# Moving a 128-byte filling tile in a Trainium2 decoder trunk: the weight pool against the pools of the moving operands

## The chip, the cores and the metric

The kernel runs on one core of one Trainium2 chip. The metric is the device time of one execution in microseconds; of several executions the median is taken. Lower is better.

## The reference

One decoder layer over a sequence of 1024 tokens and a width of 1024, all in float32:

```python
hn = rms_norm(h, norm_mix_g)
proj = hn @ w_in                      # width 10256, split into za, zb, zc, xbc, dt_raw, g_raw
ya = gmlp_mixer(za, ...)              # gated MLP over positions, in chunks of 128
yb = rg_lru_mixer(zb, ...)            # convolution, gates, linear recurrence
yc = ssd_mixer(zc, xbc, dt_raw, ...)  # Mamba-2 style chunked scan
gates = sigmoid(g_raw + b_gate)       # three gates of width 1024
merged = gates[0]*(ya @ w_branch_a) + gates[1]*(yb @ w_branch_b) + gates[2]*(yc @ w_branch_c)
h = h + merged @ w_out
hn = rms_norm(h, norm_mlp_g)
h = h + (relu(hn @ w_mlp_up)**2) @ w_mlp_down     # hidden width 4096
return rms_norm(h, final_norm_g)
```

## The kernel before

**How a product is made.** Each float32 operand is cut into a high part and a rest (`split`, lines 132 and 133: ScalarE copies the source into an fp32r tile, VectorE subtracts that from the source). A product of two operands is three fp32r matmuls on TensorE: high by high, high by rest, rest by high. Each matmul has a stationary operand of 128 by 128, brought in by a weight load of its own (the PEld rows of the profile), and a moving operand of mostly 128 by 512, streamed from SBUF. The sum is collected in PSUM. In the profile's names, `out<-moving,stationary`.

**The stages in order of time.** (1) The rows of x are normed and transposed into the `xn` pool, and the second half of za is projected with x as the stationary operand (`v_matmuls`, line 257). (2) 34 projections with a 128-column weight tile each (`wtile`, `product`, line 564): the weight's two parts come from the pool `w`, the moving operand from `xn`; the three mixers run beside them. (3) The other input projections in pairs of weight tiles by a seven-product scheme (`Pair`, `seventh`, line 487). (4) The three branch products and the gated merge (`merge_product`, line 487). (5) The output projection (`out_products`, line 1387). (6) The MLP's first product (`Super`, line 487, and `plain`, line 1647). (7) Its second product (`dn_product`, line 487), then the last norm and the stores.

```python
 46    base = ctx.enter_context(tc.tile_pool(name="base", bufs=1))
 47    wp = ctx.enter_context(tc.tile_pool(name="w", bufs=6))
 48    rawp = ctx.enter_context(tc.tile_pool(name="raw", bufs=2))
 49    small = ctx.enter_context(tc.tile_pool(name="small", bufs=1))
...
 58    xp = normed.enter_context(tc.tile_pool(name="xn", bufs=16, side="right"))
 60    pools = [acts.enter_context(tc.tile_pool(name="act", bufs=15))]
 62    halfp = mixers.enter_context(tc.tile_pool(name="half", bufs=16))
...
 84    sm(SPACER, "spacer")
...
487                mm(ps, lhs[l][kk], rhs[r][kk], start=(new and n == 0), stop=(n == 11), skip_group_check=not new)
...
564                    mm(ps[:, hsl(h)], w[wi][:, k, :], a.rhs(ai, k, h), start=(n == 0), stop=(n == 3 * KD - 1))
...
1387                mm(ps, M.tok(a, k, c), wo[nb][k][w], start=(k == 0 and a + w == 0), stop=(k == KD - 1 and a == 1))
```

**What lies where in SBUF.** The pools are stacked in the order of the code, from the left; `xn`, and `act3` in its place later, are stacked from the right end. `base` holds the identity, the ones and some columns. `w` has six tiles and `raw` two, of 4096 bytes in each partition: `w` holds weights that are already split (names `wh`, `wl`, `wt`, `wb`), `raw` holds weights as they are loaded (`raw`, `rt`). `small` holds columns of a few bytes; its first tile is `spacer`, 32 float32 values (128 bytes in each partition) that no instruction reads or writes. Behind `small` come `act`, `half`, `lruw` and `const`; later `act1`, `act2` and `actx` take the places of some of these. With the sizes in the code the pools start at these bytes of a partition:

| pool | tile names | start | start modulo 256 | modulo 512 |
|---|---|---|---|---|
| `base` | `ident`, `ones`, ... | 16512 | 128 | 128 |
| `w` | `wh`, `wl`, `wt`, `wb` | 18656 | 224 | 224 |
| `raw` | `raw`, `rt` | 43232 | 224 | 224 |
| `small`, without the spacer | ... | 51552 | 96 | 352 |
| `act`, `act2` | `a` | 52704 | 224 | 480 |
| `half`, `act1` | `h`, `c` | 114144 | 224 | 480 |
| `lruw`, `actx` | `lw`, `x` | 146912 | 224 | 480 |
| `xn`, `act3` | `xn`, `b` | 163808 | 224 | 480 |

The tiles of the large pools are 2048 or 4096 bytes long (`lruw`: 1024), and a 128-column operand within them starts at a multiple of 512 bytes.

**What sets the order.** Large parts of the program are written out in order by hand (`manual_schedule`), the rest is ordered by the framework from the data that each instruction needs. No address enters into that order.

Of the kernel before, what the change touches and what calls it, by code (L numbers as in the profile page):

```python
# [8 lines left out]
F32 = mybir.dt.float32  # L9
# [7 lines left out]
P = 128  # L17
# [13 lines left out]
SPACER = 32  # L31
# [5 lines left out]
def trunk_kernel(ctx: ExitStack, tc: tile.TileContext, x, norm_mix_g, w_in, b_gate, gmlp_ln_g, gmlp_ln_b,  # L37
# [6 lines left out]
    w_out, w_up, w_dn = w_out[0], w_mlp_up[0], w_mlp_down[0]  # L44

    base = ctx.enter_context(tc.tile_pool(name="base", bufs=1))
    wp = ctx.enter_context(tc.tile_pool(name="w", bufs=6))
    rawp = ctx.enter_context(tc.tile_pool(name="raw", bufs=2))
    small = ctx.enter_context(tc.tile_pool(name="small", bufs=1))
# [18 lines left out]
    def nm(s):  # L68
        uid[0] += 1
        return f"{s}_{uid[0]}"  # L70
# [10 lines left out]
    def sm(n, tag, dt=F32, bufs=None):  # L81
        return small.tile([P, n], dt, tag=tag, name=nm(tag), bufs=bufs)

    sm(SPACER, "spacer")

    tt = nc.vector.tensor_tensor
    stt = nc.vector.scalar_tensor_tensor
# [197 lines left out]
    with tc.manual_schedule():  # L285
# [16 lines left out]
        for c in range(2, NCH):  # L302
# [8 lines left out]
                                base=0, channel_multiplier=-1)  # L311
# [78 lines left out]
        for c in range(1, NCH):  # L390
# [23 lines left out]
            if c == 4:  # L414
                nc.gpsimd.affine_select(out=wT, in_=wT, pattern=[[0, 8], [-1, P]], compare_op=ALU.is_ge, fill=0.0,
                                        base=0, channel_multiplier=1)
# [1469 lines left out]
```

## Time and profile before

| | |
|---|---|
| median of 3 runs | 1943.36 us (1942.74 to 1943.45) |
| the profiled execution | 1942.18 us, of which 1940.5 us are the span from the first to the last instruction |
| mean granted TensorE clock | 0.995 |
| PE (matmuls) busy | 1895.9 us, 98% of the span, 8928 instructions |
| PEld (weight loads) busy | 1581.8 us, 82% |
| VectorE (DVE) / ScalarE (ACT) / GpSimd (POOL) busy | 1415.9 / 1005.3 / 259.0 us |

A matmul's row in the profile lasts longer than the distance to the next matmul's start, since matmuls overlap in the array. The pace of TensorE is therefore read from start to start, or as the length of an unbroken run of matmuls in the chain of work divided by their number, not from the mean duration of one.

### The profile page before, as it was taken

To read this page: it belongs to the slowest core of one execution; us is meant where nothing else is said; L and a number is where in the kernel's file an instruction comes from. 1 tells how busy PE (TensorE), PEld (TensorE's weight loads), DVE (VectorE), ACT (ScalarE), POOL (GpSimd) and SP (SyncE) were. 2 spreads that over 40 slices of the span, in tenths; PEclk is the share of its full clock that TensorE was granted. 3 is DMA by queue.
4 is the path that set the end of the run, shared out by engine and by line. 5 is a ranking of instruction groups with operands and counts; after the bars stand their busy time and mean duration, and the time that the engine had idled before them with its cause. 6 is when DMAs were issued, how large, how long until landed. Compare 5 with 4: busy or idle time off the path is not lost.

```text
span 1940.5 us, 23747 instructions
## 1 busy us (share of the span) xinstructions
PE 1895.9 (98%) x8928; PEld 1581.8 (82%) x8928; DVE 1415.9 (73%) x2047; ACT 1005.3 (52%) x1463; POOL 259.0 (13%) x355
## 2 busy tenths in 40 slices
PE   8999999999999999999999999999999999999996
PEld 7998888888887787878778888887788887888885
DVE  6585868787758767677777888367666567788787
ACT  6435859676534545454554544265555555343253
POOL 4112112122342010000010110000121110000000
PEclk9999999999999999999999999999999999999998
DMA  5346575575755343434398987431553458454532
GB/s 164 77 137 141 115 157 123 122 159 136 164 137 157 110 143 110 150 106 135 113 293 276 256 233 192 152 111 49 184 201 131 168 186 282 166 163 126 178 120 87
DMA packets 211015, 301.25 MB, mean 155 GB/s; under 512 B 13028, under 2 KB 125876, under 8 KB 210900
## 3 DMA queue, kind: packets, MB, share of 16 engines
q1 hardware_dynamic: 167348, 158.54, 26.6%
q0 software_dynamic: 34544, 119.69, 23.1%
q10 hardware_dynamic: 9008, 21.51, 3.1%
q8 instruction: 70, 1.15, 0.2%
q14 instruction: 45, 0.37, 0.1%
HBM read 195.75 MB, written 74.58 MB: 139 GB/s over the span
## 4 chain that ended last, share of the span: by engine, by line
PE 81%; DVE 9%; issue 4%; ACT 3%; DMA 3%; POOL 1%; ACTq 0%; SPq 0%; POOLq 0%; DVEq 0%
PE aux L487 40%; PE ps L564 16%; PE gps L487 11%; PE aux L1387 4%; PE aux L257 4%; PE aux L800 1%; DMA raw<-in_w_in_dram 1%; PE aux L736 1%; PE aux L732 1%; DVE wt L133 1%; ACT wt L132 1%; PE aux L712 1%; PE aux L1647 1%; DVE a L133 1%; PE aux L847 0%
## 5 line engine op out<-in xcount | busy, mean ns | idle before, releaser
L564 PE MATMUL ps<-xn,wh 128*128 128x512 f32 x1088 | 295.0, 392 | 0.0
L487 PE MATMUL aux<-b,b 128*128 128x512 f32 x1152 | 264.3, 389 | 0.5 <-DVE b L133 0.5
L487 PEld LDWEIGHTS aux<-b,b 128*128 128x128 f32 x1152 | 216.0, 188 | 46.5 <-DVE b L133 1.3
L564 PEld LDWEIGHTS ps<-xn,wh 128*128 128x128 f32 x1088 | 202.9, 188 | 42.2 <-issue 0.5
L487 PE MATMUL aux<-a,b 128*128 128x512 f32 x960 | 219.4, 389 | 0.0
L487 PEld LDWEIGHTS aux<-a,b 128*128 128x128 f32 x960 | 180.2, 188 | 37.4
L564 PE MATMUL ps<-xn,wl 128*128 128x512 f32 x544 | 168.2, 389 | 0.0
L487 PE MATMUL gps<-xn,wt 128*128 128x512 f32 x684 | 158.7, 389 | 2.1 <-DVE a L238 2.1
L487 PE MATMUL aux<-b,wt 128*128 128x512 f32 x672 | 156.9, 389 | 0.0
L487 PEld LDWEIGHTS gps<-xn,wt 128*128 128x128 f32 x684 | 128.3, 188 | 29.0 <-issue 2.5
L487 PEld LDWEIGHTS aux<-b,wt 128*128 128x128 f32 x672 | 126.2, 188 | 26.2
L132 ACT ACTIVATE b<-wt 128x1024 fp32r<-128x1024 f32 x88 | 90.7, 1053 | 85.6 <-DMA wt<-u_d 63.1
L133 DVE TENSOR_TENSOR wt<-a,wt 128x1024 fp32r<-128x1024 f32 x66 | 80.8, 1225 | 65.1 <-ACT wt L132 65.0
L564 PEld LDWEIGHTS ps<-xn,wl 128*128 128x128 f32 x544 | 102.1, 188 | 21.5
L133 DVE TENSOR_TENSOR b<-wt,b 128x1024 fp32r<-128x1024 f32 x88 | 107.1, 1218 | 15.7 <-ACT b L132 15.7
L1625 DVE TENSOR_TENSOR a<-aux,a 128x512 f32<-128x512 f32 x112 | 77.0, 688 | 50.4 <-PE aux L487 50.4
L133 DVE TENSOR_TENSOR a<-a,a 128x1024 fp32r<-128x1024 f32 (+1 forms) x68 | 66.5, 985 | 41.8 <-ACT a L132 41.7
L132 ACT ACTIVATE a<-a 128x1024 fp32r<-128x1024 f32 (+1 forms) x68 | 55.7, 834 | 53.0 <-DVE a L1577 45.6
L133 DVE TENSOR_TENSOR wt<-rt,wt 128x1024 fp32r<-128x1024 f32 x35 | 42.8, 1224 | 52.7 <-ACT wt L132 52.5
L487 PE MATMUL aux<-a,wt 128*128 128x512 f32 x336 | 78.7, 390 | 1.2 <-ACT a L1500 1.2
L132 ACT ACTIVATE wt<-a 128x1024 fp32r<-128x1024 f32 x66 | 69.6, 1055 | 12.5 <-DVE a L515 12.1
L487 PEld LDWEIGHTS aux<-a,wt 128*128 128x128 f32 x336 | 62.9, 188 | 15.0 <-ACT a L1500 2.0
(348 smaller groups left out, 3505.6 us busy)
## 6 DMA issues: line engine op xcount, KB each, us to landing
wt<-u_d SPq DMA_DIRECT2D x54, 512.0 KB
u_d<-a POOLq DMA_DIRECT2D x48, 512.0 KB, 4.9
raw<-in_w_in_dram SPq DMA_DIRECT2D x34, 512.0 KB
wl<-raw POOLq DMA_DIRECT2D x34, 512.0 KB, 5.2
g_d<-a POOLq DMA_DIRECT2D x24, 512.0 KB, 3.6
a<-g_d ACTq DMA_DIRECT2D x24, 512.0 KB
rt<-in_w_in_dram SPq DMA_DIRECT2D x19, 512.0 KB
a<-in_w_in_dram SPq DMA_DIRECT2D x19, 512.0 KB
```

Of the source, the lines that this page charges most:

```text
L132: actv(dst_hi, src, AF.Copy)
L133: (eng or nc.vector).tensor_tensor(out=dst_lo, in0=src, in1=dst_hi.bitcast(F32), op=ALU.subtract)
L257: mm(ps[:, :nt], X.tok(a, k, c), wk[k][w], start=(k == 0 and i == 0), stop=(k == KD - 1 and i == 2))
L487: mm(ps, lhs[l][kk], rhs[r][kk], start=(new and n == 0), stop=(n == 11), skip_group_check=not new)
L564: mm(ps[:, hsl(h)], w[wi][:, k, :], a.rhs(ai, k, h), start=(n == 0), stop=(n == 3 * KD - 1))
L712: mm(st[:, cc * 256:cc * 256 + 256], Bt[:, 2 * q + cc, :], xw[q][:, cc].rearrange("p h d -> p (h d)"), start=True, stop=True)
L732: mm(yo[:, tok(i)], pv[c // 2][:, c % 2, j * P:(j + 1) * P], Cf[:, tok(c)], start=True, stop=True)
L736: mm(yi[64 * h:64 * h + 64, tok(i)], xdt[c // 2][:, c % 2, 2 * j + h, :], E[c // 2][:, c % 2, 2 * j + h, :], start=True, stop=True)
L800: mm(ps, w[wi][:, q * P:(q + 1) * P], S["xs"][half][ai], start=(n == 0), stop=(n == 2))
L1387: mm(ps, M.tok(a, k, c), wo[nb][k][w], start=(k == 0 and a + w == 0), stop=(k == KD - 1 and a == 1))
L1625: tt(out=h, in0=ps, in1=h, op=ALU.add)
L1647: mm(ps, w[1 + l][:, k, :], f[r][k % 4], start=(n == 0), stop=(n == 3 * KD - 1))
```

## The change

The spacer is taken out of the pool `small`, which lies behind `w` and `raw`, and put into the pool `base`, which lies ahead of them. No instruction is added, removed or moved.

```diff
     base = ctx.enter_context(tc.tile_pool(name="base", bufs=1))
+    base.tile([P, SPACER], F32, name="spacer")
     wp = ctx.enter_context(tc.tile_pool(name="w", bufs=6))
     rawp = ctx.enter_context(tc.tile_pool(name="raw", bufs=2))
     small = ctx.enter_context(tc.tile_pool(name="small", bufs=1))
...
     def sm(n, tag, dt=F32, bufs=None):
         return small.tile([P, n], dt, tag=tag, name=nm(tag), bufs=bufs)
 
-    sm(SPACER, "spacer")
```

By the stacking of the pools, the tiles of `base`, `w` and `raw` start 128 bytes later (`w` at 18784 and `raw` at 43360, both 96 modulo 256). `small` is shorter by what `base` is longer, so the tiles of `small` and of all pools behind it, and those at the right end, keep their places.

## The prediction

> **What bounds the kernel now.** First the page's head, the busy times and the chain that ended last:
>
> ```profile
> span 1940.5 us, 23747 instructions
> PE 1895.9 (98%) x8928; PEld 1581.8 (82%) x8928; DVE 1415.9 (73%) x2047; ACT 1005.3 (52%) x1463; POOL 259.0 (13%) x355
> PE 81%; DVE 9%; issue 4%; ACT 3%; DMA 3%; POOL 1%; ACTq 0%; SPq 0%; POOLq 0%; DVEq 0%
> ```
>
> TensorE is busy for 98% of the span, and its matmuls make up 81% of the chain. A change of the matmuls' pace would thus reach the end nearly whole: 81% of 1940.5 us are 1572 us, and 1572 of 1895.9 us busy are 83%. So I count 83% of whatever the pace gains or loses; the rest lies where matmuls wait for operands anyhow.
>
> Next the chain in order of time (start us, length us, what), for unbroken runs of matmuls, since a run's length divided by its count is the pace:
>
> ```profile
> 83.25 37.48 PE aux L257 x240
> 143.13 32.71 PE ps L564 x144
> 676.39 10.88 PE gps L487 x48
> 1014.80 194.32 PE aux L487 x856
> 1407.05 193.44 PE aux L487 x852
> 1618.91 285.91 PE aux L487 x1260
> ```
>
> The paces at 512 columns are 32.71/144 = 227.2 ns, 10.88/48 = 226.7, 194.32/856 = 227.0, 193.44/852 = 227.0 and 285.91/1260 = 226.9. The first two runs and most of the fourth (the MLP's first product) read a stationary operand from `w` and a moving one from another pool: by the table of starts these lie 256 bytes apart modulo 512. The third and the fifth have no operand in `w`: there both lie 0 apart modulo 512. The pace is the same within 0.5 ns. The share of `w` in the fourth run, by the groups between 1407 and 1600 us (720 of about 851):
>
> ```profile
> L487 PE MATMUL aux<-b,wt 128*128 128x512 f32 x480 | 112.0, 389 | 0.0
> L487 PE MATMUL aux<-a,wt 128*128 128x512 f32 x240 | 56.0, 389 | 0.0
> ```
>
> That is the central reading: the trace holds one experiment on how the pools lie to each other, 256 bytes against 0, and it shows no effect.
>
> It doesn't hold the case of the change. Modulo 256 every pair of fp32r operands in this kernel lies 0 apart, and behind the change every pair with `w` lies 128 apart.
>
> **How many matmuls are touched.** The groups that keep shapes apart (count | busy us, mean ns | idle before):
>
> ```profile
> L564 PE MATMUL ps<-xn,wh 128*128 128x512 f32 x1088 | 295.0, 392 | 0.0
> L564 PE MATMUL ps<-xn,wl 128*128 128x512 f32 x544 | 168.2, 389 | 0.0
> L487 PE MATMUL gps<-xn,wt 128*128 128x512 f32 x684 | 158.7, 389 | 2.1 <-DVE a L238 2.1
> L487 PE MATMUL aux<-b,wt 128*128 128x512 f32 x672 | 156.9, 389 | 0.0
> L487 PE MATMUL aux<-a,wt 128*128 128x512 f32 x336 | 78.7, 390 | 1.2 <-ACT a L1500 1.2
> L487 PE MATMUL aux<-xn,wt 128*128 128x512 f32 x228 | 57.1, 399 | 0.5 <-ACT a L1003 0.5
> L487 PE MATMUL aux<-h,wt 128*128 128x512 f32 x228 | 56.7, 398 | 2.4 <-DVE wt L133 2.4
> L487 PE MATMUL gps<-h,wt 128*128 128x512 f32 x228 | 56.6, 397 | 0.0
> L1387 PE MATMUL aux<-wb,b 128*128 128x512 f32 x144 | 33.5, 389 | 0.0
> L1647 PE MATMUL aux<-b,wt 128*128 128x512 f32 x48 | 11.4, 393 | 0.0
> L1647 PE MATMUL aux<-a,wt 128*128 128x512 f32 x48 | 11.0, 389 | 0.0
> L257 PE MATMUL aux<-wb,xn 128*128 128x356 f32 x144 | 24.5, 323 | 1.0 <-DVE dtr L266 1.0
> L257 PE MATMUL aux<-h,xn 128*128 128x338 f32 x192 | 30.0, 318 | 0.0
> ```
>
> The first twelve have an operand in `w`: 1088 + 544 + 684 + 672 + 336 + 3 x 228 + 144 + 48 + 48 + 144 = 4392 matmuls. One nanosecond on each is 4.4 us, and 4.4 x 0.83 = 3.6 us at the end. That is the lever of this change.
>
> **The parts of the change.** It adds no instruction, no wait and no DMA, and moves none past another on a queue, so there is nothing to count but durations.
>
> (1) *The matmuls with `w`.* Their pace at a distance of 128 is not in the trace, so it is bounded. How much could the distance govern? The part of a matmul's time that does not grow with its columns. The run of 240 at line 257 has 48 matmuls of 356 columns and 192 of 338, on average 341.6, at 37.48/240 = 156.2 ns. Between 341.6 and 512 columns the pace grows by 70.8 ns, or 0.4155 ns a column; 512 columns are 212.7 ns, and 227.0 - 212.7 = 14.3 ns are left. Where all of it would vanish, the gain is 4392 x 14.3 ns x 0.83 = 52 us; where it would come a second time, the loss is 52 us. These are the ends of the unknown.
>
> Nearer rows exist. One is of matmuls whose operands are not 0 apart modulo 256. The mixing over positions (line 847) streams `wT`, which lies in `const` at 128 modulo 256, past a stationary `a` at 224; line 690 has both operands in `a`. Both are plain float32 with 128 columns (count: least/median/most ns):
>
> ```profile
> L847 PEld LDWEIGHTS aux<-wT,a x128: 186/192/192, 511.6 to 595.5; 128*128 128x128 f32 x128
> L847 PE MATMUL aux<-wT,a x128: 270/275/377, 511.9 to 595.7; 128*128 128x128 f32 x128
> ```
>
> ```profile
> L690 PEld LDWEIGHTS aux<-a,a x64: 190/192/192, 176.9 to 499.0; 128*128 128x128 f32 x64
> L690 PE MATMUL aux<-a,a x64: 275/275/275, 177.0 to 499.1; 128*128 128x128 f32 x64
> ```
>
> 96 bytes apart or 0, the weight load takes 192 ns and the matmul 275. Neither is an fp32r matmul of 512 columns, so they speak for the general point only. I take 0 ns, the value to which both this pair and the runs at 0 and 256 point, and keep the two ends.
>
> (2) *Splits into `w`, loads into `raw` and `w`.* VectorE reads and writes these tiles in `split`:
>
> ```profile
> L133 DVE TENSOR_TENSOR wt<-a,wt 128x1024 fp32r<-128x1024 f32 x66 | 80.8, 1225 | 65.1 <-ACT wt L132 65.0
> L133 DVE TENSOR_TENSOR wt<-rt,wt 128x1024 fp32r<-128x1024 f32 x35 | 42.8, 1224 | 52.7 <-ACT wt L132 52.5
> L133 DVE TENSOR_TENSOR b<-wt,b 128x1024 fp32r<-128x1024 f32 x88 | 107.1, 1218 | 15.7 <-ACT b L132 15.7
> L133 DVE TENSOR_TENSOR a<-a,a 128x1024 fp32r<-128x1024 f32 x34 | 41.0, 1219 | 17.3 <-ACT a L132 17.2
> ```
>
> Inputs 256 apart (the first and the third) or 0 apart (the others) take 1218 to 1225 ns. The whole spread of 7 ns on all 66 + 35 + 88 = 189 splits would be 1.3 us of an engine that has 9% of the chain, so 0.1 us there: 0. The cover is VectorE's own idle time, 27% of the span. The DMAs keep their sizes and their rows; even an effect on them would meet a queue that has 3% of the chain. 0.
>
> (3) *The tiles of `base`.* Identity and ones feed a few short matmuls and transposes, the columns are scalars of other instructions. The same 96-byte row as above covers them: 0.
>
> The sum is 0: 1942.2 us for an execution like the profiled one (1940.5 us of span and 1.7 around it), and 1943.4 for the median of the runs, which stands 1.2 us above the profiled execution.
>
> [...] The pace of fp32r matmuls is not quite fixed. Where TensorE comes out of a wait, the next steps are slower until it settles; here the timeline of TensorE behind the wait at 131.84 us (start us, length, what):
>
> ```profile
> 131.84 1.18 PE L564 MATMUL ps<-xn,wh 128*128 128x512 f32 x4
> 132.86 0.62 PE L564 MATMUL ps<-xn,wl 128*128 128x512 f32 x2
> 133.32 1.09 PE L564 MATMUL ps<-xn,wh 128*128 128x512 f32 x4
> 134.25 0.62 PE L564 MATMUL ps<-xn,wl 128*128 128x512 f32 x2
> ```
>
> From 132.86 to 134.25 us there are six steps of (1.39/6 =) 231.7 ns, 4.7 above the settled 227.0, with no releaser shown. [...]
>
> **The rivals.**
>
> *Slower: the settled pace is lost.* If weight loads and streams that lie 128 bytes apart no longer settle, the matmuls with `w` keep the unsettled pace. Place: stages 2, 3 and 6. Price: 4392 x 4.7 ns x 0.83 = 17 us, 1960.5 us; its far end is the 52 us above, 1995. It decides from 1.1 ns a matmul, where 3.6 us a nanosecond make 0.2%. For it speaks that an unsettled pace exists at all, and that all fp32r pairs of this kernel lie at one distance modulo 256, so nothing shows that others settle as well. Against it: 256 against 0 makes no difference, and the run of 852 keeps its pace although the slices of `w` that it reads lie at all multiples of 512 bytes.
>
> *Faster: the remainder of 14.3 ns shrinks.* If part of it comes from weight load and stream starting at the same place modulo 256 at the same moment, 128 bytes between them takes that away. That they start together shows in the timelines of TensorE and of its weight loads, both at 300.14 us:
>
> ```profile
> 300.14 0.39 PE L564 MATMUL ps<-xn,wl 128*128 128x512 f32 x1
> ```
>
> ```profile
> 300.14 0.87 PEld L564 LDWEIGHTS ps<-xn,wh 128*128 128x128 f32 x4
> ```
>
> The only size of such an effect in the trace is again 4.7 ns: 17 us, 1926 us; the far end is 1891. Against it speaks that the runs without `w`, at 0 modulo 512, have the same remainder as those at 256.
> [...]
>
> *The change doesn't do what it says.* If the pools were rounded to larger units, `w` would keep its distance. The time would be 1943.4, within the first case.
>
> **How the numbers follow.** About 0.2% (3.9 us) is what a measurement of this kernel can tell from no change. No change in the pace, the change without effect included: 0.45. The lost pace, 1947 to 1995: 0.32, three quarters of it below 1980. The shrunk remainder, 1891 to 1939: 0.23, half of it above 1920. The likeliest is 1943.4 us, and its own range is 1939.5 to 1947.3. The range from 1920 to 1980 holds 0.45 + 0.24 + 0.12 = 0.81. Faster 0.23, same 0.45, slower 0.32.
>
> **What would show it.** Right: the runs of the chain with `w` (lines 564 and 487 between 120 and 970 us, and from 1407 us) stay at 226.7 to 227.2 ns, the splits at 1218 to 1225, and the span at 1940.5. Slower: those same runs at 231 ns or more, while the merge (x856) and the MLP's second product (x1260) stay at 227; then the step "0 ns" of part 1 is wrong. Faster: the same runs below 226. If the runs without `w` move too, the cause is not the distance between the pools. A moved time with all paces kept would stand in the waits for the splits or the DMAs, and part 2 would be wrong.

## The result and the profile after

The changed kernel takes 1962.46 us (median of 5 runs, 1961.35 to 1963.08) against 1943.18 us before (5 runs, 1942.58 to 1943.45). The ratio is 1.0103, with a 95% interval from 1.0092 to 1.0114: it is slower by 19.3 us, or 1.0%. The profiled execution took 1961.35 us, with a span of 1959.6 us.

The page after, its head, the busy times and the chain that ended last:

```profile
span 1959.6 us, 23747 instructions
PE 1920.6 (98%) x8928; PEld 1585.9 (81%) x8928; DVE 1417.4 (72%) x2047; ACT 1003.9 (51%) x1463; POOL 258.9 (13%) x355
PE 82%; DVE 8%; issue 3%; ACT 3%; DMA 2%; POOL 1%; POOLq 0%; SPq 0%; DVEq 0%; ACTq 0%
```

The same 23747 instructions ran. TensorE is busy for 24.7 us longer, the span is 19.1 us longer, and the time in which TensorE is not busy fell from 1940.5 - 1895.9 = 44.6 us to 1959.6 - 1920.6 = 39.0 us. So all of the loss is longer matmul time, and 5.6 us of it were taken up by waits that were there anyhow (by the windows of the profile, 4.0 us of these ahead of the merge, 1.5 between the merge and the MLP's second product).

The chain in order of time, the same unbroken runs as before (start us, length us, what):

```profile
82.48 37.51 PE aux L257 x240
142.88 33.46 PE ps L564 x144
684.70 11.10 PE gps L487 x48
1027.52 194.32 PE aux L487 x856
1421.38 198.24 PE aux L487 x852
1638.05 285.91 PE aux L487 x1260
```

Divided by the counts these are 232.4 ns (227.2 before), 231.3 (226.7), 227.0 (227.0), 232.7 (227.0) and 226.9 ns (226.9) at 512 columns. The three runs that read `w` are slower by 4.6 to 5.6 ns a matmul; the merge and the MLP's second product, which have no operand in `w`, have the same length to 0.01 us. The starts give the sum by stage: the merge begins 12.7 us later than before (1027.52 against 1014.80), the run of 852 in the MLP's first product 14.3 us later, the MLP's second product 19.1 us later, and the end is 19.1 us later. Of the 4.8 us between the last two starts, all lie within the run of 852 (198.24 - 193.44).

VectorE's splits, the other thing that touches `w` and `raw`, are as before:

```profile
L133 DVE TENSOR_TENSOR wt<-a,wt 128x1024 fp32r<-128x1024 f32 x66 | 80.8, 1225 | 70.1 <-ACT wt L132 70.0
L133 DVE TENSOR_TENSOR wt<-rt,wt 128x1024 fp32r<-128x1024 f32 x35 | 42.8, 1224 | 55.2 <-ACT wt L132 55.2
```

From the starts of single matmuls in the trace, all those with `w` have a mean step of 232.5 ns (226.9 before), and all others 227.3 (226.9 before): the first nine steps behind a matmul with `w` have 230.7 (227.2 before), the later ones 226.8 in both. The steps are not evenly longer: they repeat patterns, in some stretches 232, 231, 228, 230, 233, 241 ns and in others 229 and 238 in turn, where before 95% of those with `w` were 226 or 227.

### The profile page after: what moved, and what is told of

It reads as the page before. It is cut to its first block, busy times and chain, and to the rows that moved or that the text cites. A ratio compares the mean times of both kernels' runs of the same rounds, so it can differ in the third digit from the quotient of the medians.

```text
span 1959.6 us, 23747 instructions
## 1 busy us (share of the span) xinstructions
PE 1920.6 (98%) x8928; PEld 1585.9 (81%) x8928; DVE 1417.4 (72%) x2047; ACT 1003.9 (51%) x1463; POOL 258.9 (13%) x355
## 4 chain that ended last, share of the span: by engine, by line
PE 82%; DVE 8%; issue 3%; ACT 3%; DMA 2%; POOL 1%; POOLq 0%; SPq 0%; DVEq 0%; ACTq 0%
PE aux L487 41%; PE ps L564 16%; PE gps L487 11%; PE aux L1387 5%; PE aux L257 3%; PE aux L1647 1%; PE aux L800 1%; PE aux L736 1%; DVE x L975 1%; DMA raw<-in_w_in_dram 1%; PE aux L732 1%; PE aux L712 1%; DVE wt L133 1%; DMA a<-acs_d 0%; PE aux L847 0%
## 5 line engine op out<-in xcount | busy, mean ns | idle before, releaser
L564 PE MATMUL ps<-xn,wh 128*128 128x512 f32 x1088 | 300.9, 397 | 0.0
L487 PE MATMUL aux<-b,wt 128*128 128x512 f32 x672 | 160.9, 395 | 0.0
L133 DVE TENSOR_TENSOR wt<-a,wt 128x1024 fp32r<-128x1024 f32 x66 | 80.8, 1225 | 70.1 <-ACT wt L132 70.0
L133 DVE TENSOR_TENSOR wt<-rt,wt 128x1024 fp32r<-128x1024 f32 x35 | 42.8, 1224 | 55.2 <-ACT wt L132 55.2
```

The costliest lines, as they stand in the source:

```text
L133: (eng or nc.vector).tensor_tensor(out=dst_lo, in0=src, in1=dst_hi.bitcast(F32), op=ALU.subtract)
```

## The experiments

Theory D: the distance modulo 256 between a matmul's stationary operand and its stream sets the pace. The rivals: P, the place of an operand modulo 256; R, the loads and splits of `raw`; W, only the pool `w` matters; N, other engines must be using SBUF at the same time. All times are medians; each experiment of the whole kernel is compared with runs of the kernel before on the same chip (1942.27 us beside the run with all pools moved and those at 32, 64 and 192 bytes, 1942.28 beside the other four). The two kernels of TensorE alone ran once each.

**All pools moved together.** Filling tiles of 128 bytes in `base`, in `small` and at the right end:

```diff
+    base.tile([P, 32], F32, name="spacer0")
...
+    rightp = ctx.enter_context(tc.tile_pool(name="rightsp", bufs=1, side="right"))
+    rightp.tile([P, 32], F32, name="spacer1")
     xp = normed.enter_context(tc.tile_pool(name="xn", bufs=16, side="right"))
```

> All pools with fp32r operands start 128 bytes later than before (filling tiles of 128 bytes in base, in small and at the right end), so that w, raw, act, half, xn and act3 all lie at 96 modulo 256, and no distance between them differs from before. Theory D (the distance of a matmul's two operands modulo 256 sets its pace): all matmuls of 512 columns stay at 226.7 to 227.2 ns, 1943 us. Theory P (the place of an operand modulo 256 sets it: 224 is good and 96 is bad): all 7,400 or so matmuls of 512 columns at 232.5 ns, 7400 x 5.7 ns x 0.83 = 35 us more, 1978 us.

Measured: 1942.28 us, ratio 0.9999 (0.999 to 1.0009). Its chain (each line number is 3 higher):

```profile
144.69 32.71 PE ps L567 x144
678.15 10.88 PE gps L490 x48
1409.16 193.44 PE aux L490 x852
1621.02 285.93 PE aux L490 x1260
```

`w` lies exactly where the change puts it, and the runs are as long as before the change. P is out for a move of 128 bytes: moving the other operands along with `w` takes the whole loss away. The loss belongs to the distance.

**One part of the change: `raw` alone.** The filling tile between `w` and `raw`:

```diff
+    gapp = ctx.enter_context(tc.tile_pool(name="gap", bufs=1))
+    gapp.tile([P, SPACER], F32, name="spacer0")
     rawp = ctx.enter_context(tc.tile_pool(name="raw", bufs=2))
...
-    sm(SPACER, "spacer")
```

> The filling tile stands between w and raw: raw starts 128 bytes later, w and base and all other pools as before. This is one part of the change alone. Theory D (the distance of stationary and moving operand sets the matmul's pace): raw is no operand of a matmul, so all paces stay at 227 ns, 1942 to 1943 us. Rival R (part of the 19 us comes from the loads into raw and the splits out of it): up to 19 us more, and the matmuls' pace unchanged.

Measured: 1942.22 us, ratio 1.0002 (0.9992 to 1.0011). Its run of 144 in the chain:

```profile
141.96 32.71 PE ps L565 x144
```

R is out.

**No filling tile.** `w` stays where it was, while the pools to the right of it move 128 bytes down:

```diff
-    sm(SPACER, "spacer")
```

> No filling tile at all: base, w, raw, xn and act3 as before, and act, act1, act2, half and the other pools between them 128 bytes earlier. Theory D without regard to pools: the pairs of w with half (456) and act2 (384) and the pairs of act3 with act2, act1 and act (1104 + 48 + 144 + 96) lie 128 apart and go to 232.5 ns, while w with xn and act3 (3264) and act3 with itself stay at 226.7. 2232 x 5.8 ns = 12.9 us, of which 83 to 100% on the path: 1953 to 1956 us. Rival W (it is the pool w alone that must not move): 1942 us.

Measured: 1957.46 us, ratio 1.008 (1.0065 to 1.0095). Its chain (each line number is 1 lower):

```profile
144.58 32.70 PE ps L563 x144
1021.07 195.97 PE aux L486 x856
1416.43 195.34 PE aux L486 x852
1630.21 291.48 PE aux L486 x1260
```

Now the projections (`w` with `xn`, 0 apart) keep their pace, and the runs that have no operand in `w` are longer: the MLP's second product by 5.6 us, the merge by 1.65 us. (The run of 852 is longer too: 240 of its matmuls pair `w` with `act2`, which has moved.) W is out: pairs that don't touch `w` lose as well. The time is 1.5 us above the expected range. In the starts of single matmuls the pairs at 128 average 233.0 ns, not 232.5, and the pairs at 0 that take turns with them average 227.3, not 226.9, as in the changed kernel, where the first steps behind a matmul with `w` are the longer ones (230.7 ns).

**Other distances.** `w` and `raw` are moved by 32, 64, 96, 160 and 192 bytes with the two filling tiles (for 160 and 192 the pools to the right of `small` go up by a whole 256):

```diff
+    base.tile([P, 16], F32, name="spacer0")     # 64 bytes; 8, 24, 40 and 48 for the others
...
-    sm(SPACER, "spacer")
+    sm(16, "spacer")                            # 24, 8, 56 and 48 for the others
```

> w and raw 64 bytes later than before instead of 128; all other large pools as before. Theory D in its sharp form (only a distance of 0 settles): the matmuls with w at about 232.5 ns, 1962 us. Theory D in a graded form (the cost grows with the distance up to 128): about half of the 5.7 ns, 230 ns and 1952 us. If a distance exists at which weight load and stream miss each other altogether, the matmuls with w fall below 226 ns and the time below 1939 us.

> w and raw 32 bytes later than before. Sharp form of D: 232.5 ns, 1962 us. Graded form: a quarter of the 5.7 ns, 228 ns and 1948 us.

> w and raw 192 bytes later than before, act, half and the pools behind them 256 bytes later, xn and act3 as before: the matmuls with w have their operands 64 bytes apart with the other sign modulo 256. If the distance counts without a sign, the same as with 64 bytes. If the sign counts (the weight load ahead of the stream or behind it), another pace than with 64 bytes. Both forms of D say that the runs without w stay at 227 ns, although act and act3 lie 256 bytes further apart.

> w and raw 96 bytes later than before. Theory D, by the values so far (0: 226.7, 32: 233.3, 64: 233.3, 128: 232.5, 192: 229.0 ns): between 64 and 128, about 233 ns and 1963 us. Below 226 ns, and below 1939 us, if a distance exists that is better than 0.

> w and raw 160 bytes later than before, act, half and the pools behind them 256 bytes later. Theory D, by the values so far: between 128 (232.5) and 192 (229.0), about 231 ns and 1956 us. Below 226 ns, and below 1939 us, if a distance exists that is better than 0.

The run of 852 in the chain at 32, 64, 96, 160 and 192 bytes (each line number is 1 higher):

```profile
1426.33 198.34 PE aux L488 x852
```

```profile
1424.34 198.54 PE aux L488 x852
```

```profile
1427.79 199.23 PE aux L488 x852
```

```profile
1424.87 198.70 PE aux L488 x852
```

```profile
1414.22 195.07 PE aux L488 x852
1627.73 285.91 PE aux L488 x1260
```

The last column is the mean over the whole run, in which about 720 of the 852 matmuls have an operand in `w`. Each ratio is to the runs before beside it (for the change 1943.18 us).

| `w` moved by | time, us | ratio (95%) | pace of the run of 852, ns |
|---|---|---|---|
| 0 (before) | 1942.3 | 1 | 227.0 |
| 32 | 1963.55 | 1.0109 (1.0094 to 1.0124) | 232.8 |
| 64 | 1964.43 | 1.011 (1.0093 to 1.0127) | 233.0 |
| 96 | 1968.03 | 1.0136 (1.0121 to 1.0151) | 233.8 |
| 128 (the change) | 1962.46 | 1.0103 (1.0092 to 1.0114) | 232.7 |
| 160 | 1966.11 | 1.0125 (1.0109 to 1.014) | 233.2 |
| 192 | 1951.44 | 1.0044 (1.0029 to 1.0059) | 229.0 |

The graded form of D falls: 32 bytes cost as much as 128. The sharp form in turn (232.5 ns at every distance but 0) doesn't hold at 192 bytes. The sign counts: 192 bytes up (64 down) costs less than half of 64 up. The output projection shows it within a single run, since there `w` holds the moving operand and its distance has the other sign: by the starts of single matmuls, with `w` moved by 192 the matmuls with a stationary operand in `w` take about 229 ns and the 144 of the output projection that stream from `w` 233.3; with `w` moved by 64 it is the reverse, 233.3 and 229.4. (The run of 252 in the chain that holds them takes 58.19 us at 192 bytes and 57.70 at 64, against 57.12 before.) With `w` moved by 160, by interpolation 231 ns were expected, and 233.2 came (1966.11 us against 1956); with 96, 1968.03 us against 1963. The table has no smooth course. With 192 bytes the MLP's second product keeps its 285.91 us although `act2` and `act3` lie 256 bytes further apart than before.

**The pace by itself.** A kernel of nothing but series of 96 matmuls on two tiles, whose slices start at chosen elements (`k` is `i % 12`: twelve matmuls add up to one sum):

```python
a, b = so + i % 4 * P, mo + i // 2 % 2 * 512      # so, mo: offsets of a series, in float32 elements
return dict(out=ps[i // 12 % 2][:, :w], lhsT=s[:, a:a + P], rhs=m[:, b:b + w], start=(k == 0), stop=(k == 11))
```

> None of the layer is computed: TensorE alone runs 43 series of 96 fp32r matmuls (stationary 128 by 128, moving 128 by 512, a weight load for each), while no other engine and no DMA works. The stationary operand is shifted against the moving one by 0 to 496 bytes in steps of 16, then by 4, 8, 12 and 508 bytes; then both are shifted together by 128, 16, 32 and 256 bytes, the moving one alone by 128, and at last both by 0. Each series has a line of its own. Theory D: 0 bytes 226.7 ns; 32, 64, 96, 128 and 160 bytes 232 to 234.5 ns; 192 bytes 229 ns; 256 bytes as 0; shifted together as 0. Rival N (the slower pace needs ScalarE, VectorE or DMAs that use SBUF at the same time): 226.7 ns in all series. A series below 226.7 ns would point to a layout that is faster than both kernels.

From its chain, one line for each series shown. In this order the stationary operand lies 0, 16, 32, 64, 96, 128, 160, 192, 224, 240, 256, 384 and 4 bytes behind the moving one; then both are moved by 128 bytes, both by 16, and neither:

```profile
29.78 21.76 PE ps L41 x96
51.54 21.77 PE ps L42 x96
73.30 22.39 PE ps L43 x96
118.09 22.39 PE ps L45 x96
162.75 22.48 PE ps L47 x96
207.63 22.40 PE ps L49 x96
252.44 22.39 PE ps L51 x96
296.90 21.98 PE ps L53 x96
341.27 22.40 PE ps L55 x96
363.68 21.78 PE ps L56 x96
385.46 21.76 PE ps L57 x96
563.31 22.40 PE ps L65 x96
741.14 22.30 PE ps L73 x96
830.39 21.81 PE ps L77 x96
852.20 22.19 PE ps L78 x96
940.36 21.79 PE ps L82 x96
```

Length by 96: 226.7 ns at 0, 226.8 at 16, 233.2 at 32 and at 64, 234.2 at 96, 233.3 at 128, 233.2 at 160, 229.0 at 192, 233.3 at 224, 226.9 at 240, 226.7 at 256, 233.3 at 384. N is out: TensorE alone, with no other engine at work, has the paces of the kernel within 1 ns. The whole series from 0 to 240 repeats from 256 to 496 bytes, to 0.01 us in each length. No series is below 226.7, so of the distances tried none is better at 512 columns than that of the kernel before. One part of what D expected did not come: both operands shifted together by 32, 128 or 256 bytes take 227.0 to 227.2 ns, as at 0, but shifted together by 16 bytes they take 231.1. So the distance is not all that counts; D holds for the moves by multiples of 32 bytes that were tried, and all moves of `w` here are such. And the sharp form falls here too, since 16 bytes settle (226.8 ns).

**Which two operands meet.** The same kernel with operands that alternate (32 elements are 128 bytes; the comments are added here):

```diff
+        so, mo = (v[i % 2] if isinstance(v, tuple) else v for v in (so, mo))
...
+        for i in range(N): mm(**go(i, (0, 32), (0, 32)))    # own pair 0 apart, next weight load 128 from the stream
+        for i in range(N): mm(**go(i, (32, 0), (0, 32)))    # own pair 128 apart, next weight load 0 from the stream
```

> None of the layer is computed: again TensorE alone, 96 matmuls a series, each series on a line of its own. First 0 and 128 bytes as before (226.7 and 233.3 ns by the last run). Then two series in which both operands alternate from matmul to matmul. In the first, each matmul's own operands lie 0 apart, and the stationary operand of the next matmul, whose weight load runs meanwhile, lies 128 bytes from the stream. In the second, each matmul's own operands lie 128 bytes apart and the next weight load 0 from the stream. Theory X (the weight load of the next matmul and the stream of the present one meet): 233 ns in the first and 226.7 in the second. Theory Y (a matmul's own two operands): 226.7 in the first and 233 in the second. Then 384 and 256 columns at 0 and at 128 bytes: if a load costs a fixed time, 384 columns take 53.3 ns less than 512 at both distances. Then plain float32, 512 and 128 columns, at 0 and at 128 bytes: by the prediction's nearest row no difference at 128 columns.

From its chain, in this order: 0 bytes, 128 bytes, the two series above; 384 columns at 0 and at 128 bytes; 256 columns at 0 and at 128; plain float32 with 512 columns at 0 and at 128 and with 128 columns at 0 and at 128 (the trace has two rows for each of these matmuls, so 192):

```profile
29.90 21.77 PE ps L45 x96
51.67 22.32 PE ps L46 x96
73.98 21.92 PE ps L47 x96
95.90 22.08 PE ps L48 x96
117.98 16.64 PE ps L49 x96
134.63 16.90 PE ps L50 x96
151.52 11.52 PE ps L51 x96
163.05 11.40 PE ps L52 x96
174.44 82.40 PE ps L53 x192
256.85 82.40 PE ps L54 x192
339.24 21.44 PE ps L55 x192
360.68 21.44 PE ps L56 x192
```

Both X and Y fail: the two alternating series take 228.3 and 230.0 ns, neither 226.7 nor 233. Alternating also changes the distance from one stream to the next, and this experiment can't take that apart. The rest shows where the distance matters. Plain float32 takes the same at 0 and at 128 bytes (429.2 ns a row with 512 columns and 111.7 with 128). A stream of 256 columns doesn't lose by 128 bytes, but gains a little (120.0 ns at 0, 118.8 at 128). With 384 columns the loss is 2.7 ns (173.3 and 176.0), with 512 here 5.7.

## Why the prediction was right or wrong

The time lies in the stated range, but the likeliest case, no change, did not come; the slower rival did, with its place and nearly its price. The place was rightly reasoned; that the price came so near is in part luck, as told below.

- *The central reading* (256 bytes apart or 0 makes no difference) was measured rightly and read too widely. With TensorE alone the lengths from 0 to 240 bytes come again from 256 to 496, to 0.01 us, so the two cases were one and the same distance modulo 256. The trace before held no second distance for fp32r, and the prediction said so.
- *The step that failed* is "I take 0 ns" in part 1. With it the forecast of the likeliest case falls: 0 ns a matmul was put in, and 5.6 were measured. It leaned on the plain float32 rows of lines 847 and 690 as the nearest. (Their 275 ns are lengths of rows, which are not the pace; from start to start both take 112 ns, so the comparison itself stands.) The last experiment shows that this form does not feel the 128 bytes (111.7 ns a row at 0 and at 128). The rows of the touched form with a slower pace were the unsettled steps from 132.86 us, at 231.7 ns. (Ahead of them the trace shows no wait, but four rows of plain float32 with 128 columns, lines 611 and 612, and a step of 316 ns. Behind the wait that ends at 1014.80 us the steps are 335, 231, 236, 228, 233, 231 ns and then 226 or 227.) The prediction had them, and gave the rival built on them 0.32.
- *The slower rival*: 4392 x 4.7 ns x 0.83 = 17 us forecast, 19.3 measured. The step was 5.6 ns (232.5 against 226.9), and the share at the end 19.1 of the 24.7 us of busy time, 77% and not 83%. Luck has a part in the price. Other distances cost between 2.3 ns (192 bytes) and 7.5 ns (96), and the unsettled steps are not the steps at 128 bytes: from 132.16 us before the change they run 235, 233, 236, 224, 231, 236, 228, 233, 230 ns and then settle at 226 or 227, while those at 128 repeat other patterns, and the run of 852 has 232.7 ns a step over its whole length. In the first series of TensorE alone, at distance 0, the same nine steps stand within 1 ns behind the slow steps of its start (427 ns; its 96 take 23.66 us, those of the next series 21.76), so this settling needs no other engine. That the slower pace is the unsettled one held on is not shown.
- *The remainder* of 14.3 ns, taken for the ends of the unknown (that the distance governs this part was the author's estimate): at distance 0, 384 columns take 53.3 ns more than 256 (173.3 against 120.0), and 512 take 53.4 ns more than 384 (21.77 against 16.64 us for 96). That is 0.417 ns a column, and leaves about 13 ns at each of the three. At 512 columns no distance tried takes any of it away, and the faster rival did not come; at 256 columns 128 bytes take 1.2 ns, a case that this kernel does not have.
- *TensorE alone*: a shift of the stationary operand's address against the stream's, and nothing else, moves the pace from 226.7 to 234.2 ns. With no other engine at work the paces are those of the full kernel within 1 ns (226.7 and 226.9 at 0 bytes, 233.3 and 232.5 at 128).
- *Part 2* held: the splits kept 1224 and 1225 ns, and `raw` moved alone changed nothing (1942.22 us against 1942.28). *Part 3* (the tiles of `base`) was not tested by itself.
- *The change does what it says*: the place of the loss by stages, and its return to 0 when the other pools follow `w`, show that the 128 bytes took effect.

That the settled pace depends on the distance is shown. By what mechanism it does, and whether a matmul's own stationary operand or the next one's weight load is the one that counts, was not settled.

## What to carry to other kernels

With fp32r matmuls of 512 columns, look at where the pools of stationary and moving operands start modulo 256: here, with the stream left in its place, distances of -16, 0 and 16 bytes gave the settled pace of 226.7 to 227.0 ns, while every other multiple of 16 cost 2.3 to 7.5 ns a matmul. A small tile in a pool ahead of them can shift that distance, so an edit that adds some bytes of columns can move a whole kernel: here 32 to 128 bytes cost it 1.0 to 1.4%. When a trace shows no case of the thing that is changed, take the row that shares its form of instruction before one that shares its addresses.

## What was not expected of the hardware

- The pace of TensorE alone repeats in the distance with a period of 256 bytes, and is uneven within it: 229.0 ns at 192 bytes, but 233.3 at 224 and 226.9 at 240.
- A distance of 4 bytes is not settled (232.3 ns), although 0 and 16 are (226.7 and 226.8), and both operands moved by 16 bytes, at a distance of 0, take 231.1 ns. So the place counts at 16 bytes, though not at 32, 128 or 256 (227.0 to 227.2 ns).
- The same 128 bytes gave 233.3 ns in one run of series (steps of 229 and 238 in turn) and 232.5 in the other (the longer pattern with 241). The changed kernel shows both patterns. The series before it differed, so the pattern may depend on how it is entered. This was not tested.
